# One operand of high and low tokens for every unit with channels on partitions, with the convolution's taps behind the next eviction

## The chip, the cores and the metric

The kernel runs on one core of one Trainium2 chip. A core has a matrix engine (TensorE, PE, whose weight loads are shown apart as PEld), a vector engine (VectorE, DVE), an activation engine (ScalarE, ACT), a general engine (GpSimd, POOL) and a queue engine (SyncE, SP) that here issues the loads of the weights. The metric is the device time of one execution in microseconds. Times of the kernel before: 830.33 us, the median of 3 runs (829.56 to 832.01).

## The reference

A trunk of two layers on 256 tokens of 1024 channels, in float32. Each layer normalises the stream, makes one wide input projection, runs three token mixers on parts of it, and merges them:

```python
for layer in range(DEPTH):                       # 2
    h = rms_norm(x, norm_w[layer])               # 256 x 1024
    proj = jnp.einsum('bsd,de->bse', h, w_in[layer])
    (a_xbc, a_z, a_dt, b_q, b_k, b_v, b_z,
     c_q, c_k, c_v, c_f, c_z, gates) = jnp.split(proj, split_at, axis=-1)
    y_a = mamba2_branch(a_xbc, a_z, a_dt, ...)               # branch 0
    y_b = sliding_window_branch(b_q, b_k, b_v, b_z, ...)     # branch 1
    y_c = forgetting_attention_branch(c_q, c_k, c_v, c_f, c_z, ...)  # branch 2
    branch = jnp.einsum('bsiw,iwd->bsid', jnp.stack([y_a, y_b, y_c], axis=2), w_proj[layer])
    g = jax.nn.sigmoid(gates + gate_bias[layer])
    x = x + jnp.einsum('bsd,de->bse', jnp.sum(g * branch, axis=2), w_out[layer])
return rms_norm(x, final_norm_w)
```

Branch 0 puts `a_xbc` (2048 channels: 1024 of x, 512 of B, 512 of C) through a causal convolution of four taps per channel and a SiLU, runs the chunked state-space scan (SSD) in 4 groups, adds `d_skip * x`, multiplies by `silu(a_z)` and normalises in 4 groups of 256 channels. Branch 1 rotates q and k (rope) and attends in a window of 128; branch 2 attends causally with a decay taken from `c_f`. Both are multiplied by the SiLU of their own z.

## The kernel before

**Matmuls.** A product of two float32 matrices is made of three matmuls in a fast format: weights and tokens are split into a high and a low part, and hi x high, lo x high and hi x low are added up in PSUM. Tokens' parts lie together in one tile `y.hT` (`hTh` and `hTl` are its two halves); weights arrive in pieces of 256 or 512 columns and parts of `kper` k-tiles of 128 rows (4 for 256 columns), and ACT makes `hi` of each part (L264), DVE `lo` (L265). At most `AHEAD` = 4 parts are held split; `release` frees a part and so lets the next be split and one more be loaded.

A unit is one PSUM tile of work. Units with channels on partitions (k, q, conv, z) take 128 channels by 256 tokens; units with tokens on partitions (values, gates, projections) take 128 tokens by up to 512 columns. There are two ways to compute the former. `chan` issues 24 matmuls of 256 columns and hands out the PSUM tile itself. `chan_sum` streams high and low tokens behind one another as 512 columns: 8 matmuls of hi x [high, low] and 8 of lo x high into the first half of the bank; an ACT copy (L463) brings the second half to SBUF and a DVE add (L464) adds the first half. Its matmuls alternate wide and narrow. In a layer, `chan_sum` serves the q and k of branch 2, the q of branch 1 but for its first pair, all z of branch 2 and the first four z units of branch 1: 34 units. `chan` serves the k and first q pair of branch 1 (`rotated`, where two DVE products with the rope table read PSUM), the 16 convolution units (`u_conv`), the last four z units of branch 1 and the eight of branch 0 (`u_z`, where a tanh and a DVE product read PSUM): 32 units.

**Convolution.** ACT copies the unit (L719) and makes the last tap with scale and bias (L720), both from PSUM; three DVE instructions add the other taps (L723). `end`, with the tanh (L727), the closing product (L728) and, behind every second unit of x, the launch of the SSD group, is put on the list `ends_later`.

**Order.** The instructions of TensorE are in the order of the program text as a small planner makes it: it keeps a clock of estimated TensorE time, `launch(branch, generator, delay)` puts a side task on a waiting list, `pump` (called at the end of each unit) runs those that are due, `drain(branch)` runs a branch's tasks to their end. Due times are the constants `D_...`; `D_GN1` stands between the squares of a group-norm pair and its sums on TensorE, `D_GN2` between these and the matmuls with the diagonals (L872). VectorE, ScalarE and GpSimd get their order from the scheduler of the tile framework, by the dependencies and by the place in the text. `finish(out)` (L738) places all that is on `ends_later` directly behind the eviction `out`; so a convolution's end stands behind the next unit's eviction.

The units of the first part of a layer, after values, k and q: z of branch 1 (four units), then eight pairs of convolution units (B and C first, then x), and behind each pair one light thing: the values of branch 2 twice, z of branch 1 twice, the first gates of branch 1, the first k and q of branch 2, and, behind the last pair, the first half of the projection of branch 1. An SSD group needs the cumulated decays, which DMAs issued by ACT's queue (L748) bring from DRAM to all partitions; `ds` (L764) is the first to read them. Then follow the rest of branch 1, branch 2's units, z of branch 0 with the group norm, the gates and projections of branches 0 and 2, and the output projection.

**PSUM.** Three banks `mm` (L72) serve the units in turn, five banks `mx` (L75) all else. A unit's first matmul waits until the unit three before it has been read.

Of the kernel before, what the change touches and what calls it, by code (L numbers as in the profile page):

```python
# [16 lines left out]
P = 128  # L17
# [9 lines left out]
D_GN1, D_GN2, D_CUM, D_H, D_M = 6.0, 9.0, 12.0, (4.8, 6.4), 5.0  # L27
# [17 lines left out]
def hybrid_trunk(  # L45
# [404 lines left out]
    def chan_sum(y, w, c, out):  # L450
# [3 lines left out]
        for k in range(NK):  # L454
            if k > 0:
                mm(p[:, 0:S], w.lo(k)[:, c:c + P], tokens_in_turn(y.hTh, k), start=False, stop=False)
            mm(p, w.hi(k)[:, c:c + P], y.hT[:, :, :, k, :].rearrange("p h a i -> p h i a"),
               start=(k == 0), stop=(k == NK - 1))
            if k == 0:
                mm(p[:, 0:S], w.lo(k)[:, c:c + P], tokens_in_turn(y.hTh, k), start=False, stop=False)  # L460
            if w.last and (k + 1) % w.kper == 0:
                release(w, k // w.kper + 1)
# [36 lines left out]
    def rotated(y, done, both):  # L499
# [3 lines left out]
        def u(half):  # L503
            def f(w):
                if both:
                    p = T("L1", [P, S])
                    chan_sum(y, w, half * P, p)
                    p = halves(p)
                else:
                    p = chan(y, w, half * P)  # L510
                for i in (half, 1 - half):
                    m = held[half, i] = T("L1", [P, S])
                    tt(halves(m), p, halves(cs[:, i, :]), op=ALU.mult)
# [11 lines left out]
    def u_bk(y):  # L525
# [8 lines left out]
        return rotated(y, done, False)  # L534

    def u_bq(y, g):
# [5 lines left out]
        return rotated(y, done, g > 0)  # L542
# [166 lines left out]
    def u_conv(y, u, c):  # L709
        def f(w):  # L710
            p = chan(y, w, c)
# [6 lines left out]
            x_ = T("L1", [P, S])  # L718
            act(halves(x_), p, AF.Copy)  # L719
            finish(act(halves(a), p, AF.Identity, scale=y.vec[:, 48 + u:49 + u], bias=y.vec[:, 64 + u:65 + u]))  # L720
            for j in (2, 1, 0):
                s = 3 - j
                stt(a[:, s:S], x_[:, 0:S - s], y.vec[:, 16 * j + u:16 * j + u + 1], a[:, s:S],  # L723
                    op0=ALU.mult, op1=ALU.add)
# [6 lines left out]
            ends_later.append(end)  # L731
# [6 lines left out]
    def finish(out):  # L738

        with tc.issue_after(out.ins):  # L740
            while ends_later:
# [71 lines left out]
    def u_z(y, br, u, c):  # L813
        def f(w):
            if u == 0 and br != 0:
                y.sz[br] = T("L8", [P, NK, S])
            if br == 2 or br == 1 and u < 4:
                o = y.sz[br][:, u, :]
                chan_sum(y, w, c, o)
                th = T("L1", [P, S])  # L820
                act(th, o, AF.Tanh, scale=0.5)
                y.zdone.add((br, u))
# [621 lines left out]
```

## Time and profile before

| what | value |
|---|---|
| median of 3 runs | 830.33 us (829.56 to 832.01) |
| the profiled execution, its own time | 830.05 us |
| its span, first to last instruction | 828.2 us |
| granted clock of TensorE over the span | 0.997 |
| TensorE busy | 818.4 us, 99% of the span |
| VectorE busy | 676.0 us, 82%, 1486 instructions |
| ScalarE busy | 522.7 us, 63%, 1082 instructions |
| weight splits on VectorE (L265, all forms) | 314.8 us |

The page of the profile lists the busy time of each engine, the busy tenths in 40 slices of the span, the chain of work that ended last, and the costliest groups of instructions. "Idle before" names the time in which an engine stood still ahead of a group, and what released it. The waits of an engine are listed as total, count, longest. In the timeline a row gives the start, the duration, the engine, the line and the operation, with the idle time before it in brackets; matmuls overlap, so their pace is the distance of starts. The order in which one engine executes its instructions is that of the program.

### The profile page before, as it was taken

The numbers are of one execution on the slowest core, as the hardware profiler recorded it, in microseconds if no ns is written. First come the engines' busy times: TensorE is split into PE (matmuls) and PEld (weight loads), VectorE is DVE, ScalarE is ACT, GpSimd is POOL, SyncE is SP. The second block draws the span as 40 slices with busy tenths as digits, with TensorE's granted clock in tenths as the row PEclk, the third lists the DMA queues.
The fourth block names the chain that finished last, engine by engine and source line by source line (L and its number), as shares of the span: only waits on it lengthen the run. The fifth ranks groups of instructions, "written<-read, shape, count | busy, mean of one in ns | idle before, by whom it ended". The sixth has DMA issues, their size and how long they took to land.

```text
span 828.2 us, 15796 instructions
## 1 busy us (share of the span) xinstructions
PE 818.4 (99%) x5781; PEld 743.7 (90%) x5781; DVE 676.0 (82%) x1486; ACT 522.7 (63%) x1082; POOL 97.3 (12%) x150
## 2 busy tenths in 40 slices
PE   8999999999999999999999999999999999999996
PEld 8989999988888998888999999989888889888896
DVE  6998998797997778665788989988889778795665
ACT  7767777664676767353664687767557667664442
POOL 3340000000111010210004200000002110103000
PEclk9999999999999999999999999999999999999998
DMA  9876555766655555775688455756756555476632
GB/s 312 266 206 187 164 159 152 239 214 197 191 172 172 154 167 177 251 241 184 211 269 257 131 174 176 205 158 204 248 174 196 179 167 156 136 230 228 216 104 74
DMA packets 129558, 159.38 MB, mean 192 GB/s; under 512 B 7970, under 2 KB 98202, under 8 KB 129482
## 3 DMA queue, kind: packets, MB, share of 16 engines
q1 hardware_dynamic: 114960, 140.53, 54.1%
q10 hardware_dynamic: 13690, 16.24, 6.6%
q0 software_dynamic: 832, 1.62, 0.7%
q8 instruction: 45, 0.74, 0.4%
q14 instruction: 31, 0.25, 0.1%
HBM read 154.63 MB, written 2.16 MB: 189 GB/s over the span
## 4 chain that ended last, share of the span: by engine, by line
PE 90%; DVE 4%; issue 2%; DMA 2%; ACT 1%; SPq 0%; POOLq 0%; POOL 0%; DVEq 0%; ACTq 0%
PE mm L97 79%; PE mx L97 8%; PE mx L101 4%; DVE lo L265 1%; DMA L<-cumd 1%; DMA L<-in_x_dram 1%; DVE L L723 0%; ACT hi L264 0%; DVE L L265 0%; ACT L L872 0%; DVE pp L567 0%; DVE L L259 0%; DVE L L774 0%; DVE lo L259 0%; DVE pp L585 0%
## 5 line engine op out<-in xcount | busy, mean ns | idle before, releaser
L97 PE MATMUL mm<-L,hi 128*128 128x256 f32 (+1 forms) x1568 | 362.1, 316 | 0.0
L265 DVE TENSOR_TENSOR lo<-raw,hi 128x1024 fp32r<-128x1024 f32 (+2 forms) x276 | 314.8, 1157 | 51.9 <-ACT hi L264 48.6
L264 ACT ACTIVATE hi<-raw 128x1024 fp32r<-128x1024 f32 (+2 forms) x276 | 265.8, 980 | 96.0 <-PE mm L97 83.5
L97 PE MATMUL mm<-hi,L 128*128 128x512 f32 (+2 forms) x1232 | 323.7, 352 | 0.6 <-DVE qt L464 0.4
L97 PE MATMUL mm<-L,lo 128*128 128x256 f32 x1056 | 278.3, 274 | 0.0
L97 PEld LDWEIGHTS mm<-L,hi 128*128 128x128 f32 x1568 | 258.5, 191 | 18.1 <-issue 5.1
L97 PEld LDWEIGHTS mm<-hi,L 128*128 128x128 f32 x1232 | 216.7, 190 | 24.3 <-issue 0.7
L97 PE MATMUL mm<-lo,L 128*128 128x512 f32 (+2 forms) x616 | 213.7, 349 | 0.0
L97 PEld LDWEIGHTS mm<-L,lo 128*128 128x128 f32 x1056 | 202.5, 192 | 2.8
L97 PEld LDWEIGHTS mm<-lo,L 128*128 128x128 f32 x616 | 116.4, 190 | 11.5
L936 POOL TENSOR_SCALAR_AFFINE_SELECT bias<-bias 128x128 f32<-128x128 f32 x64 | 31.0, 520 | 394.9 <-DMA bias<-cumd 377.3
L573 ACT ACTIVATE pp<-pp,nm 128x128 f32<-128x128 f32 (+1 forms) x128 | 56.5, 443 | 17.2 <-DVE nm L567 17.2
L723 DVE SCALAR_TENSOR_TENSOR L<-L,vec,L 128x255 f32<-128x255 f32 (+2 forms) x96 | 46.2, 481 | 3.8 <-ACT L L720 2.5
L585 DVE TENSOR_SCALAR pp<-pp,rsum 128x128 f32<-128x128 f32 (+1 forms) x128 | 32.2, 315 | 0.5
L463 ACT ACTIVATE L<-mm 128x256 f32<-128x256 f32 x36 | 13.7, 381 | 26.5 <-PE mm L97 26.0
L967 ACT ACTIVATE L<-L 128x512 f32<-128x512 f32 x24 | 15.1, 628 | 20.4 <-DVE L L966 20.4
L604 ACT ACTIVATE L<-mx 128x512 f32<-128x512 f32 x48 | 26.7, 596 | 0.3
L101 PE MATMUL mx<-ident,pp 128*128 128x128 f32 x192 | 26.3, 273 | 0.0
L727 ACT ACTIVATE L<-L 128x256 f32<-128x256 f32 x32 | 13.4, 418 | 18.6 <-DVE L L723 10.6
L966 DVE TENSOR_TENSOR L<-mm,L 128x512 f32<-128x512 f32 x24 | 16.4, 684 | 9.4 <-PE mm L97 8.2
L573 ACT ACTIVATION_READ_ACCUMULATOR pp<-pp,nm 128x1 f32 x128 | 24.0, 187 | 0.0
L567 DVE CUSTOM_DVE_ANT_0 pp<-mx,wmask,nsink 128x128 f32<-128x128 f32 x64 | 23.4, 411 | 0.0
(203 smaller groups left out, 767.4 us busy)
## 6 DMA issues: line engine op xcount, KB each, us to landing
raw<-in_w_in_dram SPq DMA_DIRECT2D x191, 512.0 KB, 4.7
raw<-in_w_proj_dram SPq DMA_DIRECT2D x48, 512.0 KB, 5.1
raw<-in_w_out_dram SPq DMA_DIRECT2D x16, 512.0 KB, 5.0
bias<-cumd ACTq DMA_DIRECT2D x16, 256.0 KB, 3.6
L<-cumd ACTq DMA_DIRECT2D x8, 512.0 KB, 8.0
L<-in_gate_bias_dram ACTq DMA_DIRECT2D x12, 256.0 KB
raw<-in_w_in_dram SPq DMA_DIRECT2D x4, 408.0 KB
raw<-in_w_in_dram SPq DMA_DIRECT2D x4, 384.0 KB
```

Source lines behind the costliest of these rows:

```text
L97: nc.tensor.matmul(o, a, b, **kw)
L101: nc.tensor.transpose(o, a, i)
L264: keep(act)(hi, src, AF.Copy)
L265: keep(tt)(lo, src, hi.bitcast(F32), op=ALU.subtract)
L567: nc.vector.tensor_tensor_reduce(out=pp[:, i, sl], in0=score(p, i, b), in1=biases(p, i, b), scale=-0.125, scalar=1.0e30 if ns is None else ...
L573: act(pp[:, i, sl], pp[:, i, sl], AF.Exp, scale=-1.0, bias=nm[:, e:e + 1], accum_out=sums[:, e:e + 1])
L585: ts(pp[:, i, sl], pp[:, i, sl], rs[:, 2 * i + b:2 * i + b + 1], 0.5, op0=ALU.mult, op1=ALU.mult)
L604: act(pT, pt, AF.Copy)
L723: stt(a[:, s:S], x_[:, 0:S - s], y.vec[:, 16 * j + u:16 * j + u + 1], a[:, s:S], op0=ALU.mult, op1=ALU.add)
L936: nc.gpsimd.affine_select(out=bias[:, i, dst], in_=bias[:, i, src], compare_op=ALU.is_ge, fill=NEG, base=0, pattern=[[-1, P]], channel_mul ...
L966: tt(halves(g), p, halves(y.gb), op=ALU.add)
L967: finish(act(g, g, AF.Tanh, scale=0.5))
```

## The change

All 32 units of a layer that used `chan` use `chan_sum`, so the products of the rotation, the tanh and product of z and the convolution read an SBUF tile in place of the PSUM bank. `chan_sum` itself issues in a new order: the wide matmuls of the first part, then all eight narrow ones, then the wide ones of the second part; parts are released when both kinds are done. In the convolution the ACT copy (with the DVE add behind it) is the eviction; the last tap reads SBUF too, and all four taps are put on `ends_later`, to stand behind the next unit's eviction, and they put `end` on the list in turn, which so stands behind the one after that. `finish` therefore runs only what is on the list when it begins. In `u_z` of branch 0 the order of the text is tanh, drain of the SSD tasks, product, product with x. `D_GN1` goes from 6.0 to 8.5 and `D_GN2` from 9.0 to 9.5.

```diff
--- before.py
+++ after.py
@@ -24,7 +24,7 @@
 
 D_SOFT, D_SOFT2, D_EVAC, D_SSD, D_SSD2 = 7.0, 3.0, 3.0, 8.0, 3.0
 D_K, D_Q, D_QK, D_G0, D_FOX, D_BDMA, D_BIAS, D_BC, D_SSD3 = 6.0, 5.5, 2.0, 8.0, 0.0, 4.0, 2.6, 5.5, 1.0
-D_GN1, D_GN2, D_CUM, D_H, D_M = 6.0, 9.0, 12.0, (4.8, 6.4), 5.0
+D_GN1, D_GN2, D_CUM, D_H, D_M = 8.5, 9.5, 12.0, (4.8, 6.4), 5.0
 BUDGET = 1.35
 T_PP, T_SSD, T_BIAS = 1, 1, 1
 N_RAW, N_SPLIT = 6, 6
@@ -451,15 +451,22 @@
 
 
         p = pmm()
-        for k in range(NK):
-            if k > 0:
+        ks = range(NK)
+        high = [(k, True) for k in ks]
+        low = [(k, False) for k in ks]
+
+        m = w.kper
+        seq = high[:m] + low + high[m:]
+        done = [0] * len(w.parts)
+        for n, (k, h) in enumerate(seq):
+            if h:
+                mm(p, w.hi(k)[:, c:c + P], y.hT[:, :, :, k, :].rearrange("p h a i -> p h i a"),
+                   start=(n == 0), stop=(n == len(seq) - 1))
+            else:
                 mm(p[:, 0:S], w.lo(k)[:, c:c + P], tokens_in_turn(y.hTh, k), start=False, stop=False)
-            mm(p, w.hi(k)[:, c:c + P], y.hT[:, :, :, k, :].rearrange("p h a i -> p h i a"),
-               start=(k == 0), stop=(k == NK - 1))
-            if k == 0:
-                mm(p[:, 0:S], w.lo(k)[:, c:c + P], tokens_in_turn(y.hTh, k), start=False, stop=False)
-            if w.last and (k + 1) % w.kper == 0:
-                release(w, k // w.kper + 1)
+            done[k // m] += 1
+            if w.last and done[k // m] == 2 * m:
+                release(w, k // m + 1)
         finish(act(halves(out), ordered(p[:, S:2 * S]), AF.Copy))
         tt(halves(out), ordered(p[:, 0:S]), halves(out), op=ALU.add)
 
@@ -496,21 +503,17 @@
 
 
 
-    def rotated(y, done, both):
+    def rotated(y, done):
 
         held = {}
 
         def u(half):
             def f(w):
-                if both:
-                    p = T("L1", [P, S])
-                    chan_sum(y, w, half * P, p)
-                    p = halves(p)
-                else:
-                    p = chan(y, w, half * P)
+                p = T("L1", [P, S])
+                chan_sum(y, w, half * P, p)
                 for i in (half, 1 - half):
                     m = held[half, i] = T("L1", [P, S])
-                    tt(halves(m), p, halves(cs[:, i, :]), op=ALU.mult)
+                    tt(m, p, cs[:, i, :], op=ALU.mult)
                 if half == 1:
                     done(held)
                 pump()
@@ -531,7 +534,7 @@
                 m = 32 * d
                 nc.gpsimd.dma_start(y.kT[m:P, d, :, :], y.kT[0:P - m, 0, :, :])
                 nc.gpsimd.dma_start(y.kT[0:m, d, :, :], y.kT[P - m:P, 0, :, :])
-        return rotated(y, done, False)
+        return rotated(y, done)
 
     def u_bq(y, g):
 
@@ -539,7 +542,7 @@
             q = T("qt", [P, 2, S])
             add_rotated(q, held)
             launch(1, swa_quad(y, g, q), D_Q)
-        return rotated(y, done, g > 0)
+        return rotated(y, done)
 
     def attn_quad(pair, products, biases, nsink, v, vcols, sz, gated, scored=lambda: None):
 
@@ -708,27 +711,30 @@
 
     def u_conv(y, u, c):
         def f(w):
-            p = chan(y, w, c)
+            x_ = T("L1", [P, S])
+            chan_sum(y, w, c, x_)
             if u == 8:
                 y.bcT = T("L8", [P, 8, S])
             if u == 0:
                 y.xs = T("L8", [P, 8, S])
             dst = y.xs[:, u, :] if u < 8 else y.bcT[:, u - 8, :]
             a = T("L1", [P, S])
-            x_ = T("L1", [P, S])
-            act(halves(x_), p, AF.Copy)
-            finish(act(halves(a), p, AF.Identity, scale=y.vec[:, 48 + u:49 + u], bias=y.vec[:, 64 + u:65 + u]))
-            for j in (2, 1, 0):
-                s = 3 - j
-                stt(a[:, s:S], x_[:, 0:S - s], y.vec[:, 16 * j + u:16 * j + u + 1], a[:, s:S],
-                    op0=ALU.mult, op1=ALU.add)
+
+            def taps():
+                act(a, x_, AF.Identity, scale=y.vec[:, 48 + u:49 + u], bias=y.vec[:, 64 + u:65 + u])
+                for j in (2, 1, 0):
+                    n = 3 - j
+                    stt(a[:, n:S], x_[:, 0:S - n], y.vec[:, 16 * j + u:16 * j + u + 1], a[:, n:S],
+                        op0=ALU.mult, op1=ALU.add)
+                ends_later.append(end)
+
             def end():
                 th = T("L1", [P, S])
                 act(th, a, AF.Tanh)
                 stt(dst, th, 1.0, a, op0=ALU.add, op1=ALU.mult)
                 if u < 8 and u % 2 == 1:
                     launch(0, ssd_group(y, u // 2), D_G0)
-            ends_later.append(end)
+            ends_later.append(taps)
             pump()
         return f
 
@@ -738,7 +744,7 @@
     def finish(out):
 
         with tc.issue_after(out.ins):
-            while ends_later:
+            for _ in range(len(ends_later)):
                 ends_later.pop(0)()
 
     def ssd_group(y, g):
@@ -814,29 +820,19 @@
         def f(w):
             if u == 0 and br != 0:
                 y.sz[br] = T("L8", [P, NK, S])
-            if br == 2 or br == 1 and u < 4:
-                o = y.sz[br][:, u, :]
-                chan_sum(y, w, c, o)
-                th = T("L1", [P, S])
-                act(th, o, AF.Tanh, scale=0.5)
-                y.zdone.add((br, u))
-                stt(o, th, 1.0, o, op0=ALU.add, op1=ALU.mult)
-                pump()
-                return
-            p = chan(y, w, c)
-            if u == 0 and br == 0:
+            elif u == 0:
                 y.yh[br] = T("L8", [P, 2, NK, P], F32R)
                 y.yl[br] = T("L8", [P, 2, NK, P], F32R)
+            o = T("L1", [P, S]) if br == 0 else y.sz[br][:, u, :]
+            chan_sum(y, w, c, o)
             th = T("L1", [P, S])
-            finish(act(halves(th), p, AF.Tanh, scale=0.5))
+            act(th, o, AF.Tanh, scale=0.5)
             y.zdone.add((br, u))
-            if br != 0:
-                stt(halves(y.sz[br][:, u, :]), halves(th), 1.0, p, op0=ALU.add, op1=ALU.mult)
-            else:
+            if br == 0:
                 drain(0)
-                sz = T("L1", [P, S])
-                stt(halves(sz), halves(th), 1.0, p, op0=ALU.add, op1=ALU.mult)
-                tt(y.xs[:, u, :], y.xs[:, u, :], sz, op=ALU.mult)
+            stt(o, th, 1.0, o, op0=ALU.add, op1=ALU.mult)
+            if br == 0:
+                tt(y.xs[:, u, :], y.xs[:, u, :], o, op=ALU.mult)
                 sq = T("L1", [P, S])
                 act(sq, y.xs[:, u, :], AF.Square)
                 y.sq.append(sq)
```

## The prediction

> **What bounds the kernel now.** I began with the engine table of the page, then its slices, the chain that ended last, and the waits of TensorE.
>
> ```profile
> PE 818.4 (99%) x5781; PEld 743.7 (90%) x5781; DVE 676.0 (82%) x1486; ACT 522.7 (63%) x1082; POOL 97.3 (12%) x150
> ...
> DVE  6998998797997778665788989988889778795665
> ...
> PE 90%; DVE 4%; issue 2%; DMA 2%; ACT 1%; SPq 0%; POOLq 0%; POOL 0%; DVEq 0%; ACTq 0%
> ```
>
> ```profile
> PE mx L97 <- ACT L L872: 0.4, 2, 0.2
> PE mm L97 <- DVE qt L464: 0.4, 1, 0.4
> ```
>
> TensorE (PE) is busy for 818.4 of 828.2 us, and its named waits are tenths of a microsecond. So the time is TensorE's issue time, and whatever shortens its stream is a gain as long as nobody else becomes late. The slices show who could: VectorE (DVE) stands at 8 and 9 tenths through the first part of each layer. I therefore measured that part (40 to 190, 446 to 596) and the group-norm part by windows; the columns are length, then busy time and instructions of PE, weight load, DVE, ACT and POOL, granted clock, DMA share and GB/s.
>
> ```profile
> 40.00:190.00 150.00, 149.63 (x1205) 138.28 (x1204) 137.20 (x335) 102.95 (x236) 13.06 (x20) 1.00 0.63 191
> 446.00:596.00 150.00, 150.00 (x1210) 138.86 (x1209) 137.38 (x335) 103.00 (x236) 13.26 (x19) 1.00 0.62 187
> 290.00:330.00 40.00, 39.80 (x273) 35.91 (x272) 32.23 (x76) 28.66 (x60) 4.29 (x4) 1.00 0.56 175
> 696.00:736.00 40.00, 39.80 (x272) 35.90 (x271) 32.23 (x76) 28.82 (x60) 4.29 (x4) 1.00 0.55 175
> ```
>
> In the conv part DVE has 150.00 - 137.20 = 12.8 us left; in the group-norm part it has 7.8 of 40, and ACT has over 11.
>
> **The change, part by part.**
>
> *The matmuls.* Per layer 2 units of k, 2 of the first q pair, 16 of the convolution, 4 of z of branch 1 and 8 of z of branch 0 go over: 32, so 64 in all. Each had 24 matmuls of 256 columns and gets 8 of 512 and 8 of 256; 64 x 8 = 512 matmuls go, while the columns streamed stay. Pace is read from start to start in the timeline, not from durations, since matmuls overlap.
>
> ```profile
> 69.00 0.28 PE L97 MATMUL mm<-L,lo 128*128 128x256 f32 x1
> ...
> 71.69 0.28 PE L97 MATMUL mm<-L,lo 128*128 128x256 f32 x1
> ...
> 205.89 0.38 PE L97 MATMUL mm<-lo,L 128*128 128x512 f32 x1
> ...
> 207.84 0.38 PE L97 MATMUL mm<-lo,L 128*128 128x512 f32 x1
> 208.71 0.27 PE L97 MATMUL mm<-L,lo 128*128 128x256 f32 x1
> ...
> 210.34 0.27 PE L97 MATMUL mm<-L,lo 128*128 128x256 f32 x1
> ```
>
> From 69.00 to 71.69 lie 8 steps of three narrow matmuls: 0.336 each, 0.112 a matmul, so an old unit costs 8 x 0.336 = 2.69. From 205.89 to 207.84 lie 9 wide ones of a token unit: 0.2167. From 208.71 to 210.34 lie 5 pairs of one wide and one narrow matmul, as the already converted units have them: 0.326, or 8 x 0.326 = 2.61 a unit. The new order puts wide behind wide and narrow behind narrow: 8 x 0.2167 + 8 x 0.112 = 2.63. So a converted unit saves 0.06 to 0.08, and the 68 units that only change order lose 0 to 0.02. I take 0.06 x 64 = 3.8 us of PE stream: 24 x 0.06 = 1.44 before the first projection of each layer, 8 x 0.06 = 0.48 behind it. The ends are below.
>
> The Trainium skill, page "TensorE: Matmul & The Clock Gate", section "Wait — 56ns, not 53.3ns?", gives a back-to-back matmul N / 2.4 GHz and about 2.5 ns. It speaks against the change: by it, two narrow ones cost 218.4 ns and a wide one 215.8, so 512 x 2.6 ns = 1.3 us is all there is (an estimate from that page). The token rows agree with it (216.7 ns against 215.8); the narrow rows don't (112 ns against 109.2), and the measured rows decide.
>
> *Evictions.* A converted unit was emptied by one or two readers of its PSUM bank; now ACT copies the second half and DVE adds the first.
>
> ```profile
> L464 DVE TENSOR_TENSOR L<-mm,L 128x256 f32<-128x256 f32 x36 | 15.0, 415 | 1.6 <-ACT L L463 1.4
> ...
> L463 ACT ACTIVATE L<-mm 128x256 f32<-128x256 f32 x36 | 13.7, 381 | 26.5 <-PE mm L97 26.0 <-PE mx L101 0.6
> L720 ACT ACTIVATE L<-mm,vec 128x256 f32<-128x256 f32 x32 | 18.0, 562 | 0.0
> L719 ACT ACTIVATE L<-mm 128x256 f32<-128x256 f32 x32 | 12.0, 376 | 3.7 <-PE mm L97 3.6
> ```
>
> DVE gets 64 adds of 0.415, 26.6 us, 24 of them (10.0 us) in the conv part of each layer. ACT gets 64 copies of 0.381 where the convolution's 32 old copies (0.376) fall away: 32 more, 12.2 us, in a queue with 47 us free in that part. A bank is read for 0.381 + 0.415 after the last matmul, where a convolution bank was read for 0.376 + 0.562. So it comes free about 0.14 earlier, if DVE is free. The products of the rotation and the z products read SBUF instead of PSUM, one for one, costed at nothing.
>
> *DVE's ten microseconds.* 12.8 of idle take 10.0 only if nearly all of it can be filled. The splits of the weights (low parts, 1.2 each) run ahead of their use by several microseconds, so a delay of a few microseconds there reaches no matmul; that cover is gone once DVE has lost its lead. The taps now stand behind the next eviction, so an eviction has at most one split ahead of it rather than a split and three taps. I cost the rest of the conv part at nothing, except in one place.
>
> *The first projection.* Its first bank is that of the unit three before it (the second q unit of the forgetting branch), and waits for an add queued behind the SSD's work, and that for a load of the cumulated decays:
>
> ```profile
> 150.08 0.42 ACT L727 ACTIVATE L<-L 128x256 f32<-128x256 f32 x1 [0.73 <-DVE L L723]
> 150.10 0.38 ACTq L748 DMA_DIRECT2D L<-cumd  x1
> ...
> 156.86 0.16 DVE L764 TENSOR_TENSOR ds<-L,acum 128x4 f32<-128x4 f32 x1 [3.87 <-DMA L<-cumd]
> ...
> 170.09 0.42 DVE L464 TENSOR_TENSOR qt<-mm,qt 128x256 f32<-128x256 f32 x1
> ...
> 170.57 0.48 PE L97 MATMUL mm<-hi,L 128*128 128x512 f32 x1 [0.37 <-DVE qt L464]
> ...
> 562.52 0.16 DVE L764 TENSOR_TENSOR ds<-L,acum 128x4 f32<-128x4 f32 x1 [2.95 <-DMA L<-cumd]
> ...
> 575.85 0.41 DVE L464 TENSOR_TENSOR qt<-mm,qt 128x256 f32<-128x256 f32 x1
> 576.17 0.39 PE L97 MATMUL mm<-L,hi 128*128 128x256 f32 x2
> ...
> 576.62 0.38 PE L97 MATMUL mm<-hi,L 128*128 128x512 f32 x1
> ```
>
> In the first layer DVE is solid from 156.86 to 170.51, and TensorE then waits 0.37; in the second it starts 0.36 after the add ends at 576.26. Whatever TensorE gains before this point it gives back here, unless DVE's run starts earlier or holds less. In the order of the changed program, two adds and one closing product more stand between the load and this add; a following DVE instruction starts some 0.34 after the one before it (170.09 to 170.43), so 3 x 0.34 = +1.0. Against it, the load's issue stands on ACT's queue behind the tanh of 150.08, which had waited 0.73 for taps. In the new order the last unit's taps and tanh stand behind that issue, and TensorE's stream there is by then some 20 units x 0.06 = 1.2 ahead. No row shows where the issue lands: between 0 and 1.35 earlier. I take 1.2, as the stream that launches it is what it is nearest to. DVE reaches the load later by its backlog, which may eat the 3.87 and 2.95 of waiting first. So the add ends at 170.51 + 1.0 - 1.2: -0.2 in the first layer. In the second it ends at 576.26 - 0.2 = 576.06, and with the 0.06 between add and matmul of the first layer TensorE goes on at 576.12: -0.5.
>
> *Group norm.* The two due times move the sums one unit later and the diagonals one eviction ahead of their matmuls.
>
> ```profile
> 318.91 0.38 PE L97 MATMUL mx<-L,ones 128*128 128x256 f32 x1
> 319.06 0.38 ACT L872 ACTIVATE L<-ident,sm 128x128 fp32r<-128x128 f32 x1
> ...
> 319.49 0.39 PE L97 MATMUL mx<-L,ones 128*128 128x256 f32 x1 [0.20 <-ACT L L872]
> ...
> 724.72 0.39 PE L97 MATMUL mx<-L,ones 128*128 128x256 f32 x1
> ...
> 725.30 0.39 PE L97 MATMUL mx<-L,ones 128*128 128x256 f32 x1 [0.20 <-ACT L L872]
> ```
>
> The second matmul starts 0.58 behind the first, because ACT's last diagonal ends at 319.44. Two neighbours of this width start 0.11 apart, so 0.47 goes per layer if the diagonals are ready. The ends are 0 and 0.47, and I take 0.47.
>
> *The sum.* First halves -0.2 and -0.5; second halves -(0.48 + 0.47) = -0.95 each, -1.9. Together -2.6 on the profiled run's own 830.05, so 827.45. That run lies 0.28 under the median of 830.33, which gives 827.7; I forecast 827.6.
>
> **The rivals.**
>
> *No wait at the first projection.* If DVE's backlog were small and the load some 2.4 earlier, all of TensorE's gain would last: 2 x (1.44 + 0.95), and the 0.4 of the wait: -5.2, 825.1. For it speaks that only tenths are lost there now; against it, three more DVE instructions in the solid run.
>
> *The change gives TensorE nothing.* If the wide matmul costs its 0.2167 only with tokens as the stationary side, and 0.218 here, or the blocks of eight pay at their seams, the new unit is 2.64 to 2.66, and the 68 reordered units give back what the 64 gain. Then only the two diagonals remain, -0.9: 829.4. For it speaks that the channel form has no long run of wide ones in this trace, and that the old pairs (0.326) are already cheaper than the sum of the new blocks (0.329). The rule of the page cited above would land here too.
>
> *Slower: DVE becomes the bound of the conv part.* 10.0 us of adds per layer meet 12.8 of idle, of which 3.87 (2.95) is the wait for the load, fixed in place. Of the other 8.9 (9.7) some 6.1 (7.0) must be fillable; below that the backlog outlasts the load. If half can be filled, 4.5 (4.8), DVE comes to the load 5.5 (5.2) late, 1.6 (2.2) after it landed. With the 1.0 of added work the first projection starts 2.6 late, and 2.2 + 1.0 - 0.3 = 2.9 late; second halves give back 1.9: +3.6, 833.9. For it speak the 91% of DVE in both windows and that idle behind a releaser cannot be filled by an engine that runs in order; against it, TensorE waits for DVE once in the whole trace, and the deferred taps let evictions pass.
>
> **How the numbers follow.** Chances: forecast 0.40, no wait 0.13, no gain 0.17, DVE as the bound 0.30. A difference under 0.3%, 2.5 us, can hardly be told from none here: below 827.84 is faster, above 832.82 slower. The forecast stands at that edge, so 0.23 of its 0.40 counts as faster, 0.17 as the same. Faster 0.23 + 0.13 = 0.36; of the slower case 0.04 stays under 832.82, so same 0.17 + 0.17 + 0.04 = 0.38, slower 0.26. Within the forecast the bounds are 826.6 (load 1.35 earlier, so -0.35 in the first layer, and all 1.44 kept in the second) and 830.1 (load not earlier: +1.0 in the first layer, +0.7 in the second), each with the -1.9 behind. The range reaches from the no-wait case, 825.0, to the slow one, 834.0.
>
> **What would show it.** The changed profile should have 512 matmuls fewer (5269), DVE 1550 and ACT some 32 more instructions, and DVE about 98% busy in the conv part. A converted unit should run 2.63 from its first to the next unit's first matmul. The wait for ACT L872 should be gone, and the one at the first projection should stay, at 0.4 to 2 us. A wait of TensorE for DVE's add of a convolution or z unit, or for low parts, means the slower case; wide matmuls at 0.218 mean no gain. The prediction is wrong if DVE's load wait vanishes and the first projection starts later than 170.6 or 576.6 on the span's clock.

## The result, and the profile after

The changed kernel takes 836.77 us (median of 6 runs, 835.01 to 839.38) against 830.25 of the kernel before: 1.0079 of its time, 95% interval 1.0063 to 1.0095. It is 6.5 us slower where 2.7 faster was forecast. The profiled execution took 835.01 us, 4.96 more than that of before. It is the fastest of the six, at a granted clock of 0.998; the slowest, 839.38, had 0.994. 0.4% of 836 us are 3.3, an estimate from these clocks, so a part of the 6.5 between the medians goes with a lower clock, and no trace of those executions was kept. One execution of g_pool_z1old took 1720.24 us and is not counted in its ratio.

The page of the profile after:

```profile
PE 815.7 (98%) x5269; PEld 722.7 (87%) x5269; DVE 699.4 (84%) x1550; ACT 531.4 (64%) x1114; POOL 103.5 (12%) x150
...
DVE  6999999898997788866789999999889878896665
...
PE 64%; DVE 20%; ACT 6%; issue 5%; DMA 3%; POOL 1%; SPq 0%; POOLq 0%; ACTq 0%; DVEq 0%
```

The instruction counts are as forecast, and PE's busy time fell by 2.7 us. But DVE's share of the chain that ended last rose from 4% to 20%. The waits of PE (total, count, longest):

```profile
PE mm L97 <- DVE qt L471: 4.8, 4, 1.8
PE mm L97 <- DVE L L471: 2.6, 4, 1.1
PE mx L101 <- POOL ident masks.py:199: 1.5, 1, 1.5
PE mx L97 <- DVE L L840: 1.5, 2, 0.9
```

L471 is the new add. TensorE waits 7.4 us for adds that free its banks, and 1.5 for the add of the squares ahead of a group-norm sum (L840); in the kernel before there were 0.4 and none.

Where it comes and goes, read as the distance between the two timelines at the same matmul: +0.81 at the very first unit (11.51 to 12.32, before any changed instruction, so not the change's), +4.36 at the first projection of the first layer (170.57 to 174.93), +3.66 where the second layer begins (395.13 to 398.79), +5.62 at its first projection (576.62 to 582.24), +5.1 at the end. So the first halves lost 3.55 and 1.96, the second halves gained 0.70 and 0.5.

The pace is what was forecast. A converted unit in the timeline, with the first matmul behind it:

```profile
92.60 1.03 PE L97 MATMUL mm<-L,hi 128*128 128x512 f32 x4
93.47 1.05 PE L97 MATMUL mm<-L,lo 128*128 128x256 f32 x8
94.36 1.03 PE L97 MATMUL mm<-L,hi 128*128 128x512 f32 x4
95.22 0.82 PE L101 MATMUL mx<-ident,pp 128*128 128x128 f32 x6
```

Four wide matmuls in 0.87, eight narrow ones in 0.89, four wide ones in 0.86: 2.62.

The loss has two places in the first half of a layer. The first is a bank held behind a softmax; the rows of after, then the same unit's rows of before:

```profile
112.97 0.36 ACT L470 ACTIVATE L<-mm 128x256 f32<-128x256 f32 x1
...
113.39 0.40 DVE L471 TENSOR_TENSOR L<-mm,L 128x256 f32<-128x256 f32 x1
...
113.84 0.48 PE L97 MATMUL mm<-L,hi 128*128 128x512 f32 x1 [1.10 <-DVE L L471]
```

```profile
109.71 0.36 ACT L831 ACTIVATE L<-mm 128x256 f32<-128x256 f32 x1
...
110.13 0.40 DVE L834 SCALAR_TENSOR_TENSOR L<-L,mm 128x256 f32<-128x256 f32 x1
```

The softmax came up on DVE later (its first instruction at 108.86 instead of 105.59), and with it everything queued behind: 3.26 from 110.13 to 113.39, while TensorE's stream was only 0.95 later there. The ACT copy of this bank, at 112.97, stands behind the softmax's exponentials in the same way. The second place, the load of the decays and what stands behind its first reader:

```profile
152.24 1.22 DVE L265 TENSOR_TENSOR lo<-raw,hi 128x1024 fp32r<-128x1024 f32 x1
153.38 0.48 DVE L727 SCALAR_TENSOR_TENSOR L<-L,vec,L 128x253 f32<-128x253 f32 x1
...
153.95 0.42 ACT L733 ACTIVATE L<-L 128x256 f32<-128x256 f32 x1 [2.19 <-DVE L L727]
154.00 0.38 ACTq L754 DMA_DIRECT2D L<-cumd  x1
...
160.22 0.16 DVE L770 TENSOR_TENSOR ds<-L,acum 128x4 f32<-128x4 f32 x1 [2.89 <-DMA L<-cumd]
...
161.81 0.42 DVE L471 TENSOR_TENSOR qt<-mm,qt 128x256 f32<-128x256 f32 x1
...
162.38 1.10 PE L97 MATMUL mm<-L,hi 128*128 128x512 f32 x4 [1.78 <-DVE qt L471]
...
174.36 0.42 DVE L471 TENSOR_TENSOR qt<-mm,qt 128x256 f32<-128x256 f32 x1
...
174.93 0.67 PE L97 MATMUL mm<-hi,L 128*128 128x512 f32 x2 [1.28 <-DVE qt L471]
...
562.59 0.38 ACTq L754 DMA_DIRECT2D L<-cumd  x1
...
567.53 0.16 DVE L770 TENSOR_TENSOR ds<-L,acum 128x4 f32<-128x4 f32 x1 [1.62 <-DMA L<-cumd]
...
581.68 0.42 DVE L471 TENSOR_TENSOR qt<-mm,qt 128x256 f32<-128x256 f32 x1
...
582.24 0.67 PE L97 MATMUL mm<-hi,L 128*128 128x512 f32 x2 [1.29 <-DVE qt L471]
```

Read it upwards from 162.38: TensorE waits for an add, which stands behind `ds` on DVE, which waits for the load, whose issue stands on ACT's queue behind a tanh, which waits 2.19 for a tap, which stands behind a split. The issue was at 150.10 and 556.69 before; it is 3.9 and 5.9 later, of which TensorE's own lateness explains 1.7 and 3.7, and 2.2 in each layer is left.

### The profile page after: what moved, and what is told of

The parts are those of the page before. It is cut to its first block, busy times and chain, and to the rows that moved or that the text cites. A ratio compares the mean times of both kernels' runs of the same rounds, so it can differ in the third digit from the quotient of the medians.

```text
span 833.3 us, 14824 instructions
## 1 busy us (share of the span) xinstructions
PE 815.7 (98%) x5269; PEld 722.7 (87%) x5269; DVE 699.4 (84%) x1550; ACT 531.4 (64%) x1114; POOL 103.5 (12%) x150
## 3 DMA queue, kind: packets, MB, share of 16 engines
q0 software_dynamic: 832, 1.62, 0.7%
## 4 chain that ended last, share of the span: by engine, by line
PE 64%; DVE 20%; ACT 6%; issue 5%; DMA 3%; POOL 1%; SPq 0%; POOLq 0%; ACTq 0%; DVEq 0%
PE mm L97 57%; DVE lo L265 8%; PE mx L97 5%; ACT pp L576 3%; PE mx L101 2%; DVE L L727 2%; DVE L L471 2%; DMA L<-cumd 1%; ACT hi L264 1%; POOL sm L853 1%; DVE L L516 1%; DVE L L265 1%; DMA L<-in_x_dram 1%; DVE pp L588 1%; DVE L L734 1%
## 5 line engine op out<-in xcount | busy, mean ns | idle before, releaser
L97 PE MATMUL mm<-L,hi 128*128 128x512 f32 x1056 | 267.0, 385 | 4.9 <-DVE L L471 2.6
L97 PEld LDWEIGHTS mm<-L,hi 128*128 128x128 f32 x1056 | 184.6, 190 | 31.4 <-DVE L L471 4.3
L97 PEld LDWEIGHTS mm<-L,lo 128*128 128x128 f32 x1056 | 138.4, 191 | 7.1
L97 PE MATMUL mm<-L,lo 128*128 128x256 f32 x1056 | 139.2, 275 | 0.0
L470 ACT ACTIVATE L<-mm 128x256 f32<-128x256 f32 x100 | 37.5, 375 | 38.0 <-PE mm L97 36.5
L471 DVE TENSOR_TENSOR L<-mm,L 128x256 f32<-128x256 f32 x100 | 41.6, 416 | 6.2 <-ACT L L470 5.7
L829 ACT ACTIVATE L<-L 128x256 f32<-128x256 f32 x48 | 19.8, 412 | 19.3 <-DVE L L471 19.3
L833 DVE SCALAR_TENSOR_TENSOR L<-L,L 128x256 f32<-128x256 f32 x48 | 20.3, 423 | 7.9 <-ACT L L829 7.9
L733 ACT ACTIVATE L<-L 128x256 f32<-128x256 f32 x32 | 13.2, 411 | 19.3 <-DVE L L727 14.4
L101 PEld LDWEIGHTS mx<-ident,pp 128*128 128x128 f32 x192 | 22.8, 142 | 2.6
```

What stands on the lines that cost most here:

```text
L97: nc.tensor.matmul(o, a, b, **kw)
L101: nc.tensor.transpose(o, a, i)
L470: finish(act(halves(out), ordered(p[:, S:2 * S]), AF.Copy))
L471: tt(halves(out), ordered(p[:, 0:S]), halves(out), op=ALU.add)
L833: stt(o, th, 1.0, o, op0=ALU.add, op1=ALU.mult)
```

## The experiments

The changed lines are shown shortened, each against the kernel named in the sentence or in the comment; each edit was timed in five rounds beside the kernel before. The expectations weigh two theories: by the queue theory the adds do harm by the place at which they stand in DVE's queue, by the capacity theory DVE simply has too much work.

**The change in parts.** First the matmul order alone, then convolution, branch 0's z with the due times, and rotation with branch 1's z, each with the new order and the rest as before.

```diff
-        for k in range(NK):        # chan_sum: hi0 lo0 lo1 hi1 lo2 hi2 ...
+        seq = high[:m] + low + high[m:]
```

> Only the order of wide and narrow matmuls in the already converted units changes; no engine gets other work. Queue theory (the new DVE add empties each bank from a place in an in-order queue, behind softmax work and behind the first reader of the decays) and capacity theory (DVE has simply too much work) both expect no change: 830.3, within 0.5 us. If the order itself costs (seams between blocks, weight parts released later), the time rises by 0.5 us or more.

Measured 829.44, ratio 0.9992 (0.9984 to 1.0001): no loss.

```diff
-            p = chan(y, w, c)      # u_conv
+            chan_sum(y, w, c, x_)  # taps on ends_later, end behind them
```

> New order, and only the 16 convolution units per layer converted, with their taps behind the next eviction; rotation, z and due times as before. Queue theory: the late load of the decays and the two stalls behind it (1.9 and 0.9 us in the first layer, 0.6 and 1.4 in the second) stay, the stall behind the softmax of the fourth z pair goes; 4.8 us lost less 32 x 0.06 = 1.9 gained: +2 to +3.5, 832.5 to 834. Capacity theory: 16 of 24 adds, two thirds of the loss of the whole change (+6.5): +4.5, 834.7.

Measured 833.90, ratio 1.0040 (1.0028 to 1.0053), with 3.3 us of waits for the q units' adds.

```diff
-            p = chan(y, w, c)      # u_z, branch 0 only
+            chan_sum(y, w, c, o)
-D_GN1, D_GN2, ... = 6.0, 9.0, ...
+D_GN1, D_GN2, ... = 8.5, 9.5, ...
```

> New order, the 8 z units of branch 0 per layer converted and the group norm's due times changed; convolution, rotation and z of branch 1 as before. Both theories: DVE has room there, 16 x 0.06 = 1.0 us and the two diagonal waits of 0.47 are gained: -1.0 to -1.9, 828.4 to 829.3. If the moved sums and diagonals open new waits, 830 or more.

Measured 828.99, ratio 0.9980 (0.9969 to 0.9991): faster than before. The waits for ACT's diagonals are gone, and one for the squares has come:

```profile
PE mx L97 <- DVE L L878: 1.7, 2, 0.9
```

```diff
-                if both: ... else: p = chan(y, w, half * P)   # rotated
+                chan_sum(y, w, half * P, p)
-            p = chan(y, w, c)                                 # u_z, branch 1, u >= 4
+            chan_sum(y, w, c, o)
```

> New order, and only the k and first q pair and the last four z units of branch 1 converted (8 per layer), convolution and z of branch 0 as before. Queue theory: the stall behind the softmax stays (1.1 us in the first layer, 0.9 in the second), 16 x 0.06 = 1.0 gained: +0.5 to +1.5, 830.8 to 831.8. Capacity theory: 8 of 24 adds, a third of the loss: +2.2, 832.5.

Measured 834.54, ratio 1.0051 (1.0035 to 1.0066): 8 units per layer cost as much as the 16 of the convolution (the intervals overlap), which neither theory had. The largest of its new waits is that of TensorE's transposes for the softmax's scaling on DVE:

```profile
PE mx L101 <- DVE pp L588: 1.2, 2, 0.7
```

Against e_order the parts are +4.5, +5.1 and -0.5; with the order's -0.8 they add up to 838.5; the whole took 836.8, which intervals of about 1 us each allow.

**Is it the number of adds, or where they stand?** Four edits of the changed kernel.

```diff
+        e = T("L2", [P, 2 * S])
+        finish(act(<both halves of the bank> -> e, AF.Copy))
+        gtt(out, e[:, 0:S], e[:, S:2 * S], op=ALU.add)      # POOL
```

> The changed kernel, but in all 32 newly converted units of a layer ACT copies both halves of the bank to SBUF at once (512 columns) and POOL adds them; DVE loses the 64 adds (26.6 us), POOL gets 64 of some 0.8 to 1.6 us, the bank is freed by ACT alone. Queue theory (a bank's add waits its turn behind softmax work and the decays' first reader on DVE): the DVE waits at the units go, and with them the 8.9 us; PE's 3.9 us of gain shows: 826 to 828. Capacity theory (too much DVE work delays whatever comes next): the same. If the loss comes from longer paths (sum, then taps, then tanh), not from DVE: 834 or more.

Measured 862.98, ratio 1.0393 (1.0377 to 1.0410). The edit caught more than the expectation says: all units of the rotation and of branch 1's z, 84 adds.

```profile
L473 POOL TENSOR_TENSOR L<-L 128x256 f32<-128x256 f32 x84 | 91.7, 1095 | 256.4 <-ACT L L472 214.0 <-DVE lo L265 33.7 <-ACT acum L702 4.4
```

```profile
L521 DVE TENSOR_TENSOR L<-L,cs 128x256 f32<-128x256 f32 x40 | 19.0, 518 | 14.2 <-POOL L L473 14.2
```

An add takes 1.1 us there instead of 0.42, and DVE, in order, stood still 14.2 us for the sums ahead of the rotation's products alone. Fewer DVE instructions, a longer path, 26 us lost against the changed kernel: taking the adds off DVE gains nothing where the path behind them grows. Not all of the 26 is the path: the granted clock was 0.984 to 0.995 in these executions, and some DVE instructions took longer (last section).

```diff
         finish(act(halves(out), ordered(p[:, S:2 * S]), AF.Copy))
-        tt(halves(out), ordered(p[:, 0:S]), halves(out), op=ALU.add)
+        if add:                                   # False in u_conv
+            tt(halves(out), ordered(p[:, 0:S]), halves(out), op=ALU.add)
```

> The changed kernel without the DVE add in the 16 convolution units per layer (left out: the first half of each of these banks never reaches the result, so the convolution's input is the small half alone). Everything else, order and lists too, stays. Capacity theory: 32 adds (13.3 us) fewer on DVE, most of the convolution's share goes: 832 to 833, the rest being the rotation's and branch 1's z. Queue theory: the same 32 adds are also those that hold banks, so as low; but the load of the decays still stands behind a tanh that waits for taps, so a stall at the first reader and at the first projection stays: 833 to 835.

Measured 831.07, ratio 1.0000 (0.9991 to 1.0009), below both expectations. The issue is at 150.89 here, 3.1 earlier than with the adds, while TensorE's stream is 1.5 earlier there: the adds make the tanh late, and the tanh the load.

```profile
150.89 0.38 ACTq L755 DMA_DIRECT2D L<-cumd  x1
...
158.52 0.16 DVE L771 TENSOR_TENSOR ds<-L,acum 128x4 f32<-128x4 f32 x1 [4.31 <-DMA L<-cumd]
```

```profile
PE mm L97 <- DVE qt L472: 3.5, 4, 1.6
...
PE mm L97 <- DVE L L472: 0.7, 2, 0.4
```

But `ds` starts only 1.7 earlier, 7.6 behind the issue instead of 6.2, and TensorE's waits for the q units' adds stay at 3.5 of 4.8. What goes in larger part are the waits for banks, from 2.6 to 0.7; the one behind the softmax is no longer listed. So the late load is not the only way in which these adds do harm.

```diff
-        nc.scalar.dma_start(bcg, y.cumd[...].partition_broadcast(P))
+        nc.gpsimd.dma_start(bcg, y.cumd[...].partition_broadcast(P))
```

> The changed kernel with the loads of the decays issued from POOL's queue in place of ACT's, so that they stand behind no tanh. Queue theory: the load lands some 3 us earlier, the stalls of 1.9 and 0.6 us behind its first reader go, those at the first projection (0.9, 1.4) shrink: 833 to 834.5. Capacity theory: DVE has the same work, the delay comes out at the next place: 836 to 837.

Measured 830.27, ratio 0.9997 (0.9988 to 1.0006): the whole loss is gone, with every add and every converted unit in place. Timeline, waits, and a window of the convolution part, here and in the changed kernel:

```profile
151.36 0.86 POOL L754 DMA_DIRECT2D L<-cumd  x1 [23.80 <-ACT hi L264]
...
158.24 0.16 DVE L770 TENSOR_TENSOR ds<-L,acum 128x4 f32<-128x4 f32 x1
```

```profile
PE mm L97 <- DVE L L471: 2.3, 3, 1.1
PE mx L97 <- DVE L L840: 1.7, 2, 0.9
...
PE mm L97 <- DVE qt L471: 0.6, 2, 0.4
```

```profile
40.00:190.00 150.00, 148.04 (x1041) 130.63 (x1041) 143.42 (x356) 102.26 (x238) 20.61 (x29) 1.00 0.65 191
...
40.00:190.00 150.00, 145.41 (x1029) 128.19 (x1028) 141.00 (x346) 101.35 (x236) 18.99 (x27) 1.00 0.62 187
```

The issue comes 2.6 earlier, `ds` no longer waits, and the waits for the q units' adds fall from 4.8 to 0.6. DVE is busy for 143.42 of 150 us here, against 141.00 in the changed kernel, and the kernel is no slower than before. So it is not the amount of DVE work. The waits for banks (L471) are still there, 2.3.

```diff
-            ends_later.append(taps)
+            taps()
```

> The changed kernel with the convolution's taps directly behind its own add, the end behind the next eviction as before the change. Queue theory: tanh and so the decays' load come earlier, but three taps stand ahead of more adds: between 834 and 838, and the wait of the decays' reader shows which. Capacity theory: the work is the same, no change: 836 to 837.5.

Measured 842.62, ratio 1.0138 (1.0122 to 1.0155): without the deferral the change costs about 12 us, some of it by a granted clock of 0.992 to 0.994.

```profile
PE mx L101 <- DVE pp L588: 6.1, 2, 3.0
```

```profile
157.25 0.38 ACTq L754 DMA_DIRECT2D L<-cumd  x1
```

Three taps ahead of softmax work hold TensorE's transposes, and the issue is 3.3 later still.

**The control, and what is left.** The loads on POOL's queue in the kernel before, in the rotation version, with branch 1's z back, and with `D_GN1` at 9.5.

```diff
-        nc.scalar.dma_start(bcg, ...        # the kernel before
+        nc.gpsimd.dma_start(bcg, ...
```

> The kernel before with one edit: the loads of the decays are issued from POOL's queue. The control for the run in which this edit took 6.5 us from the changed kernel. Queue theory: before the change that issue stood behind few things and TensorE lost only 0.4 us at the first projection, so at most 0.5 is gained: 829.5 to 830.5. If POOL's queue is worth some 6 us to any version of the kernel, 824 to 826, and the loss of the change has another cause.

Measured 833.04, ratio 1.0031 (1.0019 to 1.0043). POOL's queue by itself costs 2.6 us here: the loads of later groups land later, and TensorE waits for SSD products.

```profile
PE mx L97 <- DVE L L793: 2.5, 2, 1.6
```

So the edit is no general gain; with the loads on POOL's queue in both, the changed kernel is 2.8 us faster than the kernel before.

```diff
-        nc.scalar.dma_start(bcg, ...        # the version of e_rotz1
+        nc.gpsimd.dma_start(bcg, ...
```

> The version with only the rotation and the last four z of branch 1 converted (834.5 with the loads on ACT's queue), with the loads on POOL's queue. Queue theory: its loss, too, is mainly the late load, whose first reader holds DVE: 830 to 831.5. If its loss is the softmax that comes late on DVE and holds TensorE's transposes (0.55 of waiting seen per layer), the load's queue changes nothing: 833 to 835.

Measured 833.20, ratio 1.0031 (1.0020 to 1.0042), with the same 1.2 us of waiting transposes, which the load so does not cause. But the kernel before with the loads on POOL's queue took 833.04: against that this version loses nothing, where on ACT's queue it lost 4.3. Whether the load has a share in the rest of this part's loss stays open.

```diff
-            chan_sum(y, w, c, o)                 # u_z, branch 1, u >= 4, loads on POOL's queue
+            p = chan(y, w, c)
```

> The changed kernel with the loads on POOL's queue (830.3) and the last four z units of branch 1 as before the change. The wait of 1.1 and 0.8 us for the add behind the softmax goes, 8 x 0.06 = 0.5 of pace is given up: 828.4 to 829.4. If another DVE wait takes its place, 830.

Measured 832.21, ratio 1.0015 (1.0005 to 1.0025): at least no faster than with these units converted (830.27, 0.9988 to 1.0006). The wait behind the softmax shrank, and others took its place (1.7 us for q adds, 1.1 for the old z product); why was not settled.

```diff
-D_GN1, D_GN2, ... = 8.5, 9.5, ...         # loads on POOL's queue
+D_GN1, D_GN2, ... = 9.5, 9.5, ...
```

> The changed kernel with the loads on POOL's queue (830.3) and D_GN1 at 9.5 in place of 8.5, which puts the third group's sums 12 matmuls later. The two waits of 0.85 us for the add of the squares go: 828.5 to 829. If the sums only wait elsewhere, or the diagonals become late, 830.3.

Measured 832.92, ratio 1.0028 (1.0018 to 1.0039). The waits for the squares went, and the diagonals became late:

```profile
PE mx L97 <- ACT L L868: 2.0, 4, 0.8
```

**Deferral, due times, a better version.**

```diff
-            ends_later.append(end)                                  # the kernel before
+            ends_later.append(lambda: ends_later.append(end))
```

> The kernel before, with the end of each convolution unit (tanh, product, launch of the SSD group) one eviction later, as the change has it, and nothing else: no add, no converted unit, no new matmul order. Theory now: the loss arises where the decays' load is issued late and its first reader holds DVE, and the deferral alone makes the launch later: if this is the main part, the issue moves from 150.1 by 2 us or more and the time is 833 to 836. If the lateness comes from the DVE adds ahead of taps and tanh, the issue moves by a unit's launch at most and the time stays at 829.5 to 831.

Measured 830.35, ratio 0.9994 (0.9984 to 1.0003). The issue stays where it was, and the first projection's wait of 0.4 is even gone:

```profile
149.97 1.74 ACTq L748 DMA_DIRECT2D L<-cumd  x2
...
154.87 0.16 DVE L764 TENSOR_TENSOR ds<-L,acum 128x4 f32<-128x4 f32 x1 [1.45 <-DMA L<-cumd]
```

The later `end` alone makes nothing late. This run leaves the taps where they were; with taps and `end` deferred and no adds the issue was at 150.89 (f_conv_no_add), 0.8 behind the kernel before, and with the adds at 154.00.

```diff
-D_GN1, D_GN2, ... = 8.5, 9.5, ...         # the version of e_z0gn
+D_GN1, D_GN2, ... = 6.0, 9.0, ...
```

> New order, the z units of branch 0 converted, due times of the group norm as before the change (6.0 and 9.0), convolution, rotation and branch 1's z as before. With the changed due times this version took 829.0, with two waits of 0.85 us for the add of the squares in place of two of 0.47 lost to diagonals. Theory: 828.2 to 829.0, as the DVE waits go and the diagonals' come back. If the due times do not matter, 829.0.

Measured 837.02, ratio 1.0075 (1.0062 to 1.0088): 8 us more than with the new due times.

```profile
PE mx L97 <- DVE L L878: 6.1, 4, 2.1
```

The converted z has a copy and an add more ahead of tanh, products, square and sum; at the old due times the sums on TensorE wait for it. These waits are 4.4 of the 8 us; a lower granted clock is most of the rest, by an estimate (last section). The same edit on the changed kernel with the loads on POOL's queue, and on the version with convolution and branch 0's z alone:

```diff
-D_GN1, D_GN2, ... = 8.5, 9.5, ...         # the changed kernel, loads on POOL's queue
+D_GN1, D_GN2, ... = 6.0, 9.0, ...
```

> The changed kernel with the decays' loads on POOL's queue (830.3) and the due times as before the change. Theory, as in the run beside it: 829.5 to 830.3. A value of 832 or more, as with 9.5, would say that moves of a few small instructions between DVE and ACT queues are worth as much as the waits they are meant to remove.

Measured 837.42, ratio 1.0086 (1.0071 to 1.0100).

```diff
-            chan_sum(y, w, half * P, p)          # rotated; u_z of branch 1, u >= 4 alike
+            p = chan(y, w, half * P)             # also loads on POOL's queue, due times 6.0, 9.0
```

> New order, convolution and z of branch 0 converted, rotation and branch 1's z as before, old due times, the decays' loads on POOL's queue: the parts of the change that cost the least, without the late load. Theory: the pace gains 48 x 0.06 = 2.9, and small DVE waits in the convolution part of 0.5 to 1 us per layer remain: 828 to 829.5. If the POOL queue's own cost (2.8 us on the kernel before) comes with it, 831 or more.

Measured 839.00, ratio 1.0107 (1.0089 to 1.0125), with 6.0 and 6.4 us of that same wait. The second of these runs so says little about the convolution.

```diff
-D_GN1, D_GN2, ... = 6.0, 9.0, ...         # the kernel before
+D_GN1, D_GN2, ... = 8.5, 9.5, ...
```

> The kernel before with the two due times of the change and nothing else. The forecast's step: the two losses of 0.47 us to late diagonals go, 829.3. Theory now: the due times only make room for the longer chain of a converted z unit, and without it they gain at most that: 829.3 to 830.5. If moved sums or diagonals open waits of their own, 831 or more.

Measured 829.40, ratio 0.9981 (0.9972 to 0.9990): a gain, and ACT's diagonals are no longer among TensorE's waits.

```diff
-            ends_later.append(end)                                  # the version of e_z0gn
+            ends_later.append(lambda: ends_later.append(end))
```

> The best version so far (new order, z of branch 0 converted, new due times; 829.0) with the end of a convolution unit one eviction later, which took away TensorE's wait at the first projections in the kernel before. Theory: 828.3 to 829.0, ahead of both kernels. If the earlier load only moves the wait, 829.0 or more.

Measured 829.10, ratio 0.9976 (0.9967 to 0.9985): ahead of both kernels, by 2.0 and some 8 us. Its gain over the due times alone (0.9981) is within the intervals.

## Why the prediction was wrong

**The matmuls: right.** 512 fewer, 2.62 a converted unit where 2.63 was worked out, 0.06 saved each; the units of reordered `chan_sum` lost nothing that shows (e_order). The narrow matmuls go at 0.89 / 8 = 0.111 us here, as the 24 of an old unit did at 0.112. The Trainium skill, page "TensorE: Matmul & The Clock Gate", section "Wait — 56ns, not 53.3ns?", gives 0.1092 for them by its formula, an estimate; these rows, too, are above it, so the gain is larger than by that rule.

**"So it comes free about 0.14 earlier, if DVE is free": wrong by its condition.** DVE is not free. The bank that held TensorE for 1.10 is one of branch 1's z, which ended in a DVE product before the change, too; it came free 3.26 later because DVE and with it the softmax ahead of it were late, and without the convolution's adds that wait is not listed (f_conv_no_add). The sentence "I cost the rest of the conv part at nothing, except in one place" fell with it: TensorE waited 0.41 and 1.10 us in the first layer, and 0.84 in the second, ahead of that place.

**The first projection: the failed step.** The position on the queue was read rightly, the direction was not. The sum there was +1.0 for three more DVE instructions and -1.2 for an earlier load. The +1.0 held: from the start of `ds` to the end of the add it takes 14.56 (160.22 to 174.78) where it took 13.65, and 14.57 where it took 13.74 in the second layer. The -1.2 failed: the load's issue was to come between 0 and 1.35 earlier, "as the stream that launches it is what it is nearest to"; it came 3.9 later (5.9 in the second layer), and `ds` 3.36 (5.01) later. The issue hung not on TensorE's stream but on a tanh, and that on taps which DVE reached late; the bounds left no room for lateness and gave no reason for that. So the first halves, put at -0.2 and -0.5, came out at +3.55 and +1.96. That is 6.2 of the 7.6 us between 827.45 and the profiled 835.01, with the waits of the paragraph above in it; the second halves make 0.7 of the rest, the first unit 0.8.

Moving the issue to another queue takes away the whole loss (f_decays_pool), though the same edit makes the kernel before slower (g_before_pool). Removing the convolution's adds moves the issue back by 3.1, of which 1.5 is TensorE's stream (f_conv_no_add), and the later `end` without adds leaves it in place (h_late_end). The Trainium skill, page "PSUM — Partial Sum Buffer", section "Engine vs sequencer instructions", calls the queues of ACT, DVE and POOL strict first-in, first-out. The trace agrees: the issue at 154.00 starts 0.05 behind the start of the tanh that had waited 2.19, and on DVE nothing starts in the 2.89 that `ds` waits.

**The slower rival: right in sign, too small (+3.6, 833.9, where the medians differ by 6.5), half right in mechanism.** Its price was that of a delayed reader of the load and a late first projection, which is what happened. Its cause, idle time that cannot hold 10 us of adds, is not what cost the time: DVE was to come to the load after it had landed, but it still waited for the load, 2.89 and 1.62, and was 94% busy in the conv part (141.00 of 150) rather than about 98%. With the same adds and the load elsewhere it is 95.6% busy and no time is lost. What decides is not how much DVE does but what time-critical work hangs on an instruction queued behind an add. Of the signs that were named, TensorE's wait for DVE's add of a z unit came, and the first projections started late (174.93 and 582.24), while DVE's wait for the load did not vanish.

**Group norm: the gain was right, its use wrong.** The due times alone gain 0.19% (i_gn_only), 1.6 us where 2 x 0.47 was put. But they were costed as a part by itself, when they are the cover for the longer chain of the converted z: in the changed kernel they go into that, with 1.5 us of waits left over; without them 7 to 8 us are lost (h_z0, h_pool_gnold), part of it by a lower granted clock. The second halves gained 0.70 and 0.5 rather than 0.95.

**What stays open.** The rotation and branch 1's z cost 4.3 us alone and nothing with the loads on POOL's queue in both; 1.2 of the 4.3 are the waiting transposes, which are there in both cases, and the rest was not traced to a cause. How much of the 6.5 between the medians is a lower clock is only estimated: the two profiled executions of the changed kernel and of f_decays_pool, at 0.998 and 0.999, differ by 4.8. And with the loads on POOL's queue, putting z back gained nothing (g_pool_z1old): each edit also changes the order in which the scheduler places DVE's and ACT's instructions, and these runs do not separate that from the edit.

## What to carry to other kernels

When an eviction gets a step more on an engine that runs in order, don't ask whether the engine has room; follow what hangs on the longer path, and look above all for a DMA issue that stands in a compute engine's queue behind something that waits. A due time is worth what it covers: cost it together with the chain that it leaves time for, not as a change of its own. And where a term depends on when something is issued, bound it by the engine that feeds the instruction ahead of it, on the late side too.

## What the runs showed of the hardware

While POOL added (f_pool_add), a DVE instruction with two SBUF inputs took longer: the first tap 662 ns on average, against 479 in the changed kernel.

```profile
L732 DVE SCALAR_TENSOR_TENSOR L<-L,vec,L 128x255 f32<-128x255 f32 x32 | 21.2, 662 | 4.3 <-ACT L L729 3.6
```

```profile
L727 DVE SCALAR_TENSOR_TENSOR L<-L,vec,L 128x255 f32<-128x255 f32 x32 | 15.3, 479 | 0.5
```

The Trainium skill, page "SBUF — State Buffer", section "SBUF: two separate sides", says that such an instruction and a GpSimd one that reads SBUF lock one port pair against each other for a whole instruction. The trace agrees. Of the 32 first taps 12 took 946 to 1026 ns, each beside a POOL add that ended some 0.28 us before the tap did; the other 20 took 469 to 505. A tap beside an add, and one without:

```profile
82.00 1.52 POOL L473 TENSOR_TENSOR L<-L 128x256 f32<-128x256 f32 x1
82.86 0.95 DVE L732 SCALAR_TENSOR_TENSOR L<-L,vec,L 128x255 f32<-128x255 f32 x1
...
86.10 0.48 DVE L732 SCALAR_TENSOR_TENSOR L<-L,vec,L 128x255 f32<-128x255 f32 x1
```

The second and third taps in that run kept 0.48 to 0.49 on average.

Where TensorE waited long in the group-norm part, the granted clock (the third number from the end of a row) was lower too: 0.96 over 40 us in both layers of h_z0, where TensorE was busy for 36.98, against 1.00 and 39.15 in e_z0gn.

```profile
290.00:330.00 40.00, 36.98 (x214) 31.86 (x213) 30.99 (x78) 27.53 (x62) 5.20 (x4) 0.96 0.46 147
```

```profile
290.00:330.00 40.00, 39.15 (x234) 34.47 (x233) 32.82 (x78) 29.90 (x63) 5.93 (x4) 1.00 0.53 170
```

Two such stretches cost 2 x 0.04 x 40 = 3.2 us, an estimate from these rows; with 4.4 of waits that is most of the 8 us between the two versions. It does not follow always: in h_pool_gnold the first layer had the same 36.98 at a clock of 1.00, the second 36.98 at 0.96. What sets it off these runs do not show.
